# A second branch's product in seven half-size products, and gated output weights made early and kept in DRAM

## The chip, the cores and the metric

The kernel runs on one core of a Trainium2 chip. The metric is the device time of one execution in microseconds (us); a kernel's time is the median of several executions. Before the change it is 1652.44 us (three runs, 1652.39 to 1654.09).

## The reference

One layer of a two-branch backbone, with 1024 latent tokens, 256 context tokens and a model width of 1024, all in float32:

```python
pl = project(modulate(x, sh_x, sc_x), w_in)          # one wide input projection, split into 11 streams
o_gla  = bidir_gla(q, k, v, la_f, la_b, s_f, s_b)    # branch A: gated linear attention, both directions
o_diff = diff_attention(...)                         # branch B: difference of two softmaxes, 8 heads
a = merge_heads(rms_norm(o_gla) * gla_gain) * silu(gla_gate)
b = merge_heads(rms_norm(o_diff) * diff_gain * (1 - lam_init)) * silu(diff_gate)
y = sigmoid(m_gla) * (a @ w_br_gla) + sigmoid(m_diff) * (b @ w_br_diff)
x = x + g_x * (y @ w_out)
```

The change concerns `b @ w_br_diff` (the second branch's product), and `w_out` with its gate `g_x`, which the kernel multiplies into the columns of `w_out`.

## The kernel before

**Arithmetic.** A float32 product is made of three matmuls in a reduced format: each operand is split into a high part (a copy by ACT, the `ACTIVATE` rows) and a low part (a subtraction by DVE), and `mm3` adds hi·hi, hi·lo and lo·hi into one PSUM bank. A half tile of 128 x 512 outputs over the full depth of 1024 is 8 blocks of 128 by 3 matmuls, 24 in all; a full product of two 1024 x 1024 matrices is 16 half tiles, or 384 matmuls.

**Seven products.** The kernel already makes some large products from half-size blocks in seven half-size products instead of eight: both sides are cut into 2 x 2 blocks of 512, sums of blocks are formed, and seven products of these (48 matmuls each, 336 in all) are added up into the four output blocks.

**Stages.** Each stage writes what the next needs to DRAM.
- Projections (`phase_a`) fill the first half millisecond. In the paired-product stage (about 200 to 481 us; `pair_weights` and `pairs`) three groups of columns of `w_in` (`gv`, `dv`, `dg`) are made in seven products each. The token side comes from DRAM in 128 x 1280 tiles `g<-d_s`, the weights in 128 x 2 x 512 tiles `raw` and `l`; `pair_weights` forms and splits the weight sums on DVE and ACT. `direct` takes the results of one of the seven products out of PSUM.
- Gated linear attention, then the differential attention up to about 1454 us. Its scores are the `s` tiles, its transposes and value products the `b` tiles, its exponentials the `e` tiles.
- The tail, from there to the end: the second branch's product, the merge of both branches, and the output product in seven half-size products (`phase_c`).

**What sets the order.** All instruction streams are static. When the program is built, a `Driver` plays all tasks against estimated costs and writes each engine's instructions down in the order in which its model would run them, ready tasks by priority (a lower number first). All DMAs go through SP, in order; `store` queues a transfer to DRAM once its source is made. On the chip each engine follows its list and waits on semaphores. A pool tag (`raw`, `yf`, `wt`, ...) is a set of on-chip tiles; a task waits in `acq` for a free one.

**Filler.** During attention PE would wait for ACT and DVE, so `fill` lays half tiles of other products between the score and value matmuls: first gates (kind 0), then `a @ w_br_gla` (kind 1), then what it can of the second branch (kind 2). They use the PSUM banks `mb` and, from the end of the scores on, `mc`. When a half tile is done, `post` on DVE takes it out of PSUM into a tile `ft` (priority `PP`, which is -1), and only then can the bank be used again. Kind 2 is started by `first_two`, has its operand `b` split by `splits` from the tiles `wr<-d_bT`, and its results finished by `post_y`, which reads the gates and the first branch's half by `load_y`.

**Output product.** In `phase_c`, `left` makes the sums of `y` (operands `y11` to `s4`), `right` loads blocks of `w_out`, multiplies them on DVE by the gate `gb` (which made a round trip through `d_gb` in DRAM), forms their sums and splits them (`w11`, `w21`, `t2`, `t1`, `t3`, `t4`, `w22`).

In the profile L335 is a matmul, L361 a transpose on PE, L197 any operation on ACT, DVE or POOL, and L300 a DMA.

Of the kernel before, what the change touches and what calls it, by code (L numbers as in the profile page):

```python
# [20 lines left out]
P = 128  # L21
# [207 lines left out]
class Hybrid:  # L229
# [18 lines left out]
        ya=("sbC", 8), yb=("sbC", 8), yc=("sbC", 8), yf=("sbC", 16), sf=("sbC", 2), o=("sbC", 4), gbo=("sbC", 1), wr=("sbC", 8),  # L248
# [141 lines left out]
    def scratch(self):  # L390
# [13 lines left out]
        self.d_gb = d("d_gb", [P, 2, 512])  # L404
# [340 lines left out]
    def job_gate(self):  # L745
# [5 lines left out]
        for n in range(2):  # L751
# [27 lines left out]
            self.rel("p", self.pool.tensor_scalar(gb[:, n], bias, 0.5, 0.0, ALU.mult, ALU.add))  # L779
        self.store([(self.d_gb, gb)], ("gb", 1), ev=self.ev_gb)  # L780
# [139 lines left out]
    def pair_weights(self, cols, ev_load, ev_run):  # L920
# [8 lines left out]
        ev_l = {(g, n, kk): Event() for g in range(len(cols)) for n, kk, _ in LOADS}  # L929

# [12 lines left out]
        def run():  # L943
            yield ev_run
            for g in range(len(cols)):
# [31 lines left out]
                for n, o in (("t1", "w22"), ("t3", "w12"), ("t4", "w21"), ("v22", "v22")):  # L977
                    for k in range(4):
                        yield ev_l[g, o, k // 2]
                        e = yield from operand(n, k, blk(o, k))  # L980
                        if k % 2:
                            self.rel(slots[g, o, k // 2][0], e)
            d.set(self.ev_pw)

        d.spawn(load(), prio=3)
        d.spawn(run(), prio=3)
        return wp

# [146 lines left out]
    def direct(self, g, t, pm, tag):  # L1135
# [801 lines left out]
    DT = (0, 4, 1, 5, 2, 6, 3, 7)  # L1937
# [88 lines left out]
    def fill(self):  # L2026
# [4 lines left out]
               [(1, s, a["w_br_gla"][0], s * P) for s in range(8)] + \  # L2031
               [(2, s, a["w_br_diff"][0], s * P) for s in self.DT]
# [11 lines left out]
        def conv(n, raw):  # L2044
            yield self.ev_b2
            yield from self.acq("wt", 2)
            hi = self.t("wt", [P, NK, P], F32R)
# [29 lines left out]
        def half_tile(n, half, rhs):  # L2077
# [7 lines left out]
            if kind == 1:  # L2085
                yield from self.acq("ft")
                mt = self.t("ft", [P, 512])
                self.dma(mt, self.d_m[0][s][:, half * 512:(half + 1) * 512])
            elif kind == 2:
                d.spawn(self.load_y(s, half), prio=-1)  # L2090
            x = [0, None]

            def step():
# [3 lines left out]
                if k == NK - 1:  # L2097
# [40 lines left out]
        def splits():  # L2138
            r = Rhs([[[None] * 2 for _ in range(NK)] for _ in range(2)])
            r.ev = {(k, half): Event() for k in range(NK) for half in range(2)}  # L2140

            def one(k, half, x):
                yield from self.acq(f"h{half}", 2)
                hi, lo = (self.t(f"h{half}", [P, 512], F32R) for _ in range(2))
                r[0][k][half], r[1][k][half] = hi, lo
                yield d.on("ACT", x)
                self.act.activation(hi, x, AF.Copy)
                yield d.on("DVE", hi)
                e = self.dve.tensor_tensor(lo, x, hi.bitcast(F32), ALU.subtract)
                self.rel("wr", e)  # L2150
                d.set(r.ev[k, half], e)

            def run():
                yield self.ev_c2
                for half in range(2):
                    for k in range(NK):
                        yield self.ev_bT[k]
                        yield from self.acq("wr")
                        x = self.t("wr", [P, 512])
                        self.dma(x, self.d_bT[k][:, half * 512:(half + 1) * 512])  # L2160
                        d.spawn(one(k, half, x), prio=-2)
            d.spawn(run(), prio=-2)
            return r

# [6 lines left out]
        while n < len(todo):  # L2171
            kind = todo[n][0]
            one = kind == 2 or todo[n][:2] in ((1, 6), (1, 7))
            two = [n] if one else [n, n + 1]
            end = all(t[0] != kind for t in todo[n + len(two):])
            if kind == 2 and todo[n][1] == self.DT[0]:
                yield self.ev_c
                yield from self.first_two(evs[n:n + 2], (lambda m: ws[n + m]), rhs)
                n += 2
                continue  # L2180
            for half in range(2):
# [4 lines left out]
                if end:  # L2186
# [3 lines left out]
                    if half == 0 and kind == 1:  # L2190
                        nxt = splits()
            n += len(two)
            if end:
                rhs = nxt
        d.set(self.ev_fill)

    def first_two(self, evs, ws, rhs):

        d = self.d
        pms = []  # L2200
        yield self.ev_aT[7, 7, 2]
        for x in range(4):
            yield from self.acq("mc")
            pms.append(self.t("mc", [P, 512]))
        order = [(0, k, m) for m in range(2) for k in range(NK - 1)] + [(0, NK - 1, 0), (0, NK - 1, 1)]
        for half, k, m in order + [(1, k, m) for m in range(2) for k in range(NK)]:
            yield evs[m][0]
            if k == 0:
                d.spawn(self.load_y(self.DT[m], half), prio=-1)
            yield rhs.ev[k, half]  # L2210
            hi, lo = ws(m)
            e = self.mm3(pms[2 * m + half], hi[:, k], lo[:, k], rhs[0][k][half], rhs[1][k][half], k == 0, k == NK - 1)
            yield AtPE(0)
            if k == NK - 1:
                d.spawn(self.post_y("mc", self.DT[m], half, pms[2 * m + half]), d.when(pms[2 * m + half]), prio=-1)
                if half:
                    self.rel("wt", e, 2)

    def phase_b(self):
# [3 lines left out]
        self.ev_c, self.ev_c2, self.ev_s2 = Event(), Event(), Event()  # L2223
# [30 lines left out]
    def load_y(self, dt, half):  # L2254

        cs = slice(half * 512, (half + 1) * 512)
        yield self.ev_c2
        yield from self.acq("o")
        my = self.t("o", [P, 2, 512])
        self.dma(my[:, 0], self.d_m[1][dt][:, cs])  # L2260
        self.dma(my[:, 1], self.d_y[dt][:, cs])
        self.ev_my[dt, half].t_ = my
        self.d.set(self.ev_my[dt, half])

    def post_y(self, tg, dt, half, pm):

        yield self.ev_my[dt, half]
        my = self.ev_my[dt, half].t_
        yield self.d.when(my)
        e = self.dve.scalar_tensor_tensor(my[:, 0], my[:, 0], 1.0, pm, ALU.add, ALU.mult)  # L2270
        self.rel(tg, e)
        y = self.y[dt, half] = self.t("yf", [P, 512])
        e = self.dve.tensor_tensor(y, my[:, 0], my[:, 1], ALU.add)
        self.rel("o", e)
        self.d.set(self.ev_y[dt, half], e)

    def phase_c(self):
        a, d = self.a, self.d
        wo = a["w_out"][0]
        self.y = {}  # L2280
        self.ev_y = {(dt, half): Event() for dt in range(8) for half in range(2)}
        self.ev_my = {(dt, half): Event() for dt in range(8) for half in range(2)}

        def to_c():
# [9 lines left out]
            yield self.ev_gb  # L2294
            self.gb = self.t("gbo", [P, 2, 512])
            self.dma(self.gb, self.d_gb)
# [21 lines left out]
        def operand(ev, tag, src, then=()):  # L2318
# [5 lines left out]
            def run():  # L2324
# [3 lines left out]
                for f in then:  # L2328
                    f(e)
            d.spawn(run(), prio=-2)  # L2330

        def left():
# [3 lines left out]
            def take(n, tag, k, src, then=()):  # L2336
                yield from self.acq(tag, 2)
                operand(ev_l[n, k], tag, src, then)

            for k in range(4):  # L2340
                for c, n, tag in ((0, "y11", "ya"), (1, "y12", "yb")):
                    yield self.ev_y[4 * c + k, 0]
                    yield from take(n, tag, k, y(0, c, k))
                for c in range(2):
# [18 lines left out]
        def right():  # L2363

            w = {}

            def gate(n, k):
                x = w[n, k]
                self.dve.tensor_tensor(x, x, self.gb[:, int(n[2]) - 1], ALU.mult)

            def op(k, o, x, y, f):
                self.dve.tensor_tensor(w[o, k], w[x, k], w[y, k], f)

            def load(n, k, x):
                w[n, k] = x
                r, c = (int(n[1]) - 1) * 512 + k * P, (int(n[2]) - 1) * 512
                self.dma(x, wo[r:r + P, c:c + 512])

            def early():
                for k in range(4):  # L2380
                    yield self.ev_y[self.DT[k // 2], k % 2]
                    for n in ("w22", "w12"):
                        yield from self.acq("wr")
                        load(n, k, self.t("wr", [P, 512]))
                for k in range(4):
                    for n in ("w22", "w12"):
                        yield d.on("DVE", w[n, k])
                        gate(n, k)
                    op(k, "w12", "w22", "w12", sub)
                    d.set(ev_e[k])  # L2390

            ev_e = [Event() for _ in range(4)]
# [125 lines left out]
```

## Time and profile before

| | |
|---|---|
| time, median of three runs | 1652.44 us (1652.39 to 1654.09) |
| profiled execution | 1653.85 us, span 1652.1 us, mean granted TensorE clock 0.997 |
| PE busy | 1627.2 us (98%), 8389 matmuls and transposes |
| DVE, ACT, POOL busy | 1162.3 us (70%), 798.9 us (48%), 595.4 us (36%) |
| DMA | 294.44 MB, 178 GB/s over the span |

PE is TensorE's matmuls, PEld its weight loads, DVE VectorE, ACT ScalarE, POOL GpSimd, SP SyncE, which issues the DMAs. The profile is one execution; its time minus its span is what lies around the program. A row of a timeline gives start, duration, engine and operation, and in brackets the engine's idle time before it with what ended that. A row of groups gives busy time and mean duration in ns, then the idle time before. A row of windows gives busy time of each engine in a stretch of the span with the instruction count, then the granted clock, the busy share of the DMA engines, and GB/s. The chain of waits is followed back from the last instruction; its rows give start, duration and what ran.

### The profile page before, as it was taken

To read this page: it belongs to the slowest core of one execution; us is meant where nothing else is said; L and a number is where in the kernel's file an instruction comes from. 1 tells how busy PE (TensorE), PEld (TensorE's weight loads), DVE (VectorE), ACT (ScalarE), POOL (GpSimd) and SP (SyncE) were. 2 spreads that over 40 slices of the span, in tenths; PEclk is the share of its full clock that TensorE was granted. 3 is DMA by queue.
4 is the path that set the end of the run, shared out by engine and by line. 5 is a ranking of instruction groups with operands and counts; after the bars stand their busy time and mean duration, and the time that the engine had idled before them with its cause. 6 is when DMAs were issued, how large, how long until landed. Compare 5 with 4: busy or idle time off the path is not lost.

```text
span 1652.1 us, 24253 instructions
## 1 busy us (share of the span) xinstructions
PE 1627.2 (98%) x8389; PEld 1355.0 (82%) x8389; DVE 1162.3 (70%) x2019; ACT 798.9 (48%) x1640; POOL 595.4 (36%) x649
## 2 busy tenths in 40 slices
PE   8999999999999999999999999999999999999999
PEld 3788888888788888888888888888888788888887
DVE  4697853355567687687772798888888888538594
ACT  4666523343434545546442666666666656422141
POOL 1510210000146565464640455555555656600000
PEclk9999999999999999999999999999999999999999
DMA  8557857687674576546458155445356743277422
GB/s 301 180 194 260 296 212 246 235 282 272 217 227 147 176 209 183 175 148 191 116 148 232 58 130 136 118 112 135 107 139 202 225 128 97 90 233 267 154 76 77
DMA packets 248970, 294.44 MB, mean 178 GB/s; under 512 B 20712, under 2 KB 169104, under 8 KB 248848
## 3 DMA queue, kind: packets, MB, share of 16 engines
q1 hardware_dynamic: 248848, 292.90, 56.1%
q8 instruction: 66, 1.08, 0.3%
q14 instruction: 56, 0.46, 0.1%
HBM read 199.51 MB, written 93.32 MB: 177 GB/s over the span
## 4 chain that ended last, share of the span: by engine, by line
PE 88%; DVE 5%; DMA 3%; ACT 2%; issue 1%; POOL 0%; SPq 0%; DVEq 0%; ACTq 0%
PE mm L335 31%; PE mc L335 11%; PE mb L335 9%; PE s L335 8%; PE b L335 6%; PE tp L335 5%; PE b L361 4%; PE go L335 4%; PE gs L335 4%; PE gt L335 4%; DVE sm L197 2%; PE tp L361 2%; DMA raw<-in_w_in 1%; PE mz L335 1%; ACT e L197 1%
## 5 line engine op out<-in xcount | busy, mean ns | idle before, releaser
L335 PE MATMUL mm<-w,h 128*128 128x512 f32 x1260 | 318.3, 401 | 0.6 <-DVE w L197 0.4
L335 PEld LDWEIGHTS mm<-w,h 128*128 128x128 f32 x1260 | 231.8, 188 | 47.5 <-DVE w L197 1.0
L197 DVE TENSOR_REDUCE sm<-s 128x1 f32<-128x1024 f32 (+1 forms) x192 | 192.9, 1040 | 42.5 <-PE s L335 39.5
L197 ACT ACTIVATE e<-s,sm 128x1280 f32<-128x1280 f32 x128 | 170.1, 1331 | 88.4 <-DVE sm L197 68.8
L335 PE MATMUL mb<-h,wt 128*128 128x512 f32 x744 | 201.6, 406 | 0.0
L197 POOL TENSOR_SCALAR at<-ac 128x512 fp32r<-128x512 f32 x128 | 98.4, 769 | 248.1 <-ACT ac L197 225.4
L335 PE MATMUL s<-hk,aq 128*128 128x512 f32 (+1 forms) x768 | 176.1, 364 | 5.2 <-ACT e L197 4.5
L197 POOL TENSOR_TENSOR at<-ac,at 128x512 fp32r<-128x512 f32 x128 | 173.4, 1355 | 10.7
L335 PEld LDWEIGHTS mb<-h,wt 128*128 128x128 f32 x744 | 131.1, 189 | 22.5 <-ACT ft L197 0.2
L335 PE MATMUL mm<-h,w 128*128 128x512 f32 x576 | 140.1, 398 | 2.7 <-ACT p L197 0.9
L335 PEld LDWEIGHTS s<-hk,aq 128*128 128x128 f32 x768 | 121.2, 189 | 22.3 <-ACT e L197 6.0
L335 PE MATMUL mc<-h,wt 128*128 128x512 f32 x600 | 138.5, 390 | 0.0
L335 PE MATMUL b<-at,vv 128*128 128x256 f32 x960 | 132.7, 287 | 1.0 <-ACT ac L197 0.8
L335 PEld LDWEIGHTS mm<-h,w 128*128 128x128 f32 x576 | 108.2, 191 | 27.6 <-DVE w L197 1.3
L335 PEld LDWEIGHTS mc<-h,wt 128*128 128x128 f32 x600 | 111.9, 188 | 22.7
L335 PEld LDWEIGHTS b<-at,vv 128*128 128x128 f32 x960 | 121.2, 190 | 3.6 <-ACT ac L197 1.0
L197 POOL TENSOR_TENSOR sm<-sm,nhalf 128x2 f32<-128x2 f32 (+2 forms) x94 | 114.5, 1218 | 14.2 <-DVE sm L197 8.8
L197 DVE SCALAR_TENSOR_TENSOR e<-e,sm,e 128x1280 f32<-128x1280 f32 x64 | 116.8, 1824 | 1.5
L197 ACT ACTIVATE ac<-b 128x512 f32<-128x512 f32 x120 | 71.6, 598 | 82.7 <-PE b L361 82.6
L197 DVE TENSOR_TENSOR w<-raw,w 128x512 fp32r<-128x512 f32 x120 | 85.8, 737 | 30.7 <-ACT w L197 29.7
L197 ACT ACTIVATE w<-raw 128x512 fp32r<-128x512 f32 x120 | 72.3, 628 | 69.8 <-DVE raw L197 23.5
L197 POOL TENSOR_TENSOR p<-p,gdif 128x512 f32<-128x512 f32 x12 | 16.2, 1358 | 241.5 <-DVE p L197 210.4
(283 smaller groups left out, 2908.3 us busy)
## 6 DMA issues: line engine op xcount, KB each, us to landing
raw<-in_w_in SPq DMA_DIRECT2D x63, 512.0 KB, 4.5
g<-d_s SPq DMA_DIRECT2D x32, 640.0 KB, 5.5
aq<-d_qT SPq DMA_DIRECT2D x128, 128.0 KB, 3.4
d_dv<-pl SPq DMA_DIRECT2D x40, 256.0 KB, 2.2
gv<-d_v SPq DMA_DIRECT2D x40, 256.0 KB, 3.1
d_kT<-pl SPq DMA_DIRECT2D x40, 256.0 KB, 2.6
hk<-d_kT SPq DMA_DIRECT2D x32, 320.0 KB, 5.3
vv<-d_dv SPq DMA_DIRECT2D x16, 640.0 KB, 7.3
```

What stands on the lines that cost most here:

```text
L197: self.ins = f(out, *args, **kw).ins
L335: self.ins = self.nc.tensor.matmul(out, lhsT, rhs, start=start, stop=stop, skip_group_check=more).ins
L361: self.nc.tensor.transpose(out, src, self.ident[:n, :n])
```

## The change

Four things change.

1. **The second branch's product in seven.** Kind 2 leaves `fill`, and `first_two`, `splits`, `load_y` and `post_y` go. Instead `prepare` loads the blocks of `w_br_diff` (a11 to a22, rows of 2 KB) and of `b` (b11 to b22, from `d_bT`), forms eight sums for each of four blocks on DVE and splits fourteen operands for each block; `diff` runs seven products of 48 matmuls over them, taken out of PSUM by `copy` (ACT), `finish` and `rest` (DVE). The products are, in order, a11·b11, a12·b21, s2·t2, s1·t1, s3·t3, a22·t4 and s4·b22.
2. **`w_out` made early.** A new task `presums` runs in the paired-product stage, after the weight operands of the first group (two blocks), of the second (one) and of the third (one). For each block it loads four 128 x 512 pieces of `w_out`, gates them by `gb`, forms the four sums (eight DVE operations) and stores seven results to `d_pre`. In the tail `right` only loads these and splits them. `gb` stays on chip.
3. **`direct` for `dv`.** The PSUM tile is copied out by ACT first, and split from the copy.
4. **Priorities and tiles.** `post` of kind 1 goes from priority -1 to -4. `yf` has 8 tiles instead of 16, a new tag `yg` has 8, and `gbo` goes.

The core of the diff:

```diff
         ya=("sbC", 8), yb=("sbC", 8), yc=("sbC", 8),
-        yf=("sbC", 16), sf=("sbC", 2), o=("sbC", 4), gbo=("sbC", 1), wr=("sbC", 8),
+        yf=("sbC", 8), yg=("sbC", 8), sf=("sbC", 2), o=("sbC", 4), wr=("sbC", 8),
...
+    WIN = ((0, 1), (2,), (3,))
+    def presums(self, ev_win):
...
+        def out(x11, x12, x21, x22, put):
+            yield self.ev_gbt
+            for n, y in (("w11", x11), ("w21", x21), ("w22", x22), ("w12", x12)):
+                yield d.on("DVE", y)
+                dve.tensor_tensor(y, y, self.gb[:, int(n[2]) - 1], mult)
+                if n != "w12":
+                    put(n, y)
+            yield from op(x12, x22, x12, sub)
+            yield put("t3", x12, "w11")
+            yield from op(x11, x12, x11, add)
+            yield put("t2", x11, "w21")
+            yield from op(x21, x21, x11, sub)
+            yield put("t4", x21, "w22")
+            yield from op(x22, x22, x11, sub)
+            put("t1", x22)
+        for win, blocks in zip(ev_win, self.WIN):
+            yield win
+            for k in blocks:
...
+                for tag in ("l5", "x4"):
+                    yield from self.acq(tag)
+                    tiles[tag] = self.t(tag, [P, 2, 512])
...
+                for y, r, c in zip(x, (0, 0, 1, 1), (0, 1, 0, 1)):
+                    self.dma(y, src[r * 512 + k * P:r * 512 + (k + 1) * P, c * 512:(c + 1) * 512])
...
     def direct(self, g, t, pm, tag):
...
+        yield from self.acq("p")
+        x = self.t("p", [P, 512])
+        self.rel(tag, self.act.activation(x, pm, AF.Copy))
...
-        e = yield from self.split(pm, hi, lo)
-        self.rel(tag, e)
+        e = yield from self.split(x, hi, lo)
+        self.rel("p", e)
...
     def fill(self):
...
-               [(1, s, a["w_br_gla"][0], s * P) for s in range(8)] + \
-               [(2, s, a["w_br_diff"][0], s * P) for s in self.DT]
+               [(1, s, a["w_br_gla"][0], s * P) for s in range(8)]
...
-                    if kind == 2:
-                        d.spawn(self.post_y(tg, s, half, pm), e, prio=-1)
-                    else:
-                        d.spawn(post(tg, kind, s, half, pm, mt), e, prio=self.PP)
+                    d.spawn(post(tg, kind, s, half, pm, mt), e, prio=-4 if kind else self.PP)
...
+        yield self.ev_c
+        yield from self.diff()
...
+    DA = ("a11", "a12", "s2", "s1", "s3", "a22", "s4")
+    DB = ("b11", "b21", "t2", "t1", "t3", "t4", "b22")
+    ORDER = ("b11", "b12", "b22", "a12", "b21", "a21", "a22")
...
+    def prepare(self):
+        OPS = (("S1", "a21", "a21", "a22", add, ("l_a21", "l_a22"), 2), ("S2", "a11", "a21", "a11", sub, ("S1", "a11"), 2),
+               ("S4", "a12", "a12", "a11", sub, ("S2", "a12"), 4), ("S3", "a11", "a22", "a11", sub, ("S4", "s2"), 4),
+               ("T3", "b12", "b22", "b12", sub, ("l_b12", "l_b22"), 2), ("T2", "b11", "b12", "b11", add, ("T3", "b11"), 2),
+               ("T4", "b21", "b21", "b11", sub, ("T2", "b21"), 3), ("T1", "b11", "b22", "b11", sub, ("T4", "t2"), 3))
...
+    def diff(self):
...
+        todo = ((0, True, "copy", 0, 0), (1, True, "add", 0, 0), (0, False, "copy", 1, 0), (0, False, "copy", 1, 1),
+                (1, True, "keep", 1, 1), (1, False, "add", 1, 0), (0, False, "last", 0, 1))
+        for n, (b, new, what, r, c) in enumerate(todo):
+            for t in range(4):
...
+                for k in range(4):
+                    yield self.ev_d[self.DA[n], k]
+                    yield self.ev_d[self.DB[n], k]
...
+                    e = self.mm3(pm, lh[:, cs], ll[:, cs], rh, rl, k == 0 and new, k == 3, not new)
...
         def right():
+            yield self.ev_raw
+            for n in RIGHT:
                 for kk in range(2):
...
+                    self.dma(x, self.d_pre[n][:, 2 * kk:2 * kk + 2])
...
+                        operand(ev_r[n, 2 * kk + j], "h0", x[:, j])
```

The static order also shows what the diff does not. The first place is PE late in the attention, at one pair's scores (`s`), in the kernel before; `b<-ident,e` are transposes and `mb<-h,wt` filler of kind 1:

```order
L335 MATMUL s_1691_8515<-hk_8271,aq_13145 128x512 x4
L361 MATMUL b_2820_13577<-ident,e_2714_13158 128x128 x4
L335 MATMUL s_1691_8515<-hk_8271,aq_13389 128x512 x4
L361 MATMUL b_2824_13602<-ident,e_2714_13158 128x128 x4
L361 MATMUL b_2827_13611<-ident,e_2714_13158 128x128 x2
L361 MATMUL b_2830_13619<-ident,e_2735_13247 128x128 x4
L335 MATMUL mb_13635<-h_2644_12867,wt_13311 128x512
```

The same engine and place in the changed kernel, up to the middle of the stretch (the next `s`, of `aq_13488`, comes after nine more `mb` rows and four transposes):

```order
L335 MATMUL s_1704_8614<-hk_8370,aq_13244 128x512 x4
L335 MATMUL mb_13671<-h_2657_12966,wt_13410 128x512
L335 MATMUL mb_13671<-h_2658_12968,wt_13410 128x512
L335 MATMUL mb_13671<-h_2657_12966,wt_13411 128x512
L335 MATMUL mb_13671<-h_2659_12970,wt_13410 128x512
L335 MATMUL mb_13671<-h_2660_12972,wt_13410 128x512
L335 MATMUL mb_13671<-h_2659_12970,wt_13411 128x512
L361 MATMUL b_2835_13687<-ident,e_2727_13257 128x128 x4
```

Fifteen filler matmuls now stand between these two `s` groups, where none stood. The DVE rows of the same place, before; `ft<-ft,mb` is the `post` that frees the bank `mb`:

```order
L197 SCALAR_TENSOR_TENSOR e_2797_13485<-e_2803_13529,sm_13550,e_2797_13485 128x1280
L197 TENSOR_SCALAR sm_13466<-sm_13466,sm_13464 128x1
L197 TENSOR_TENSOR b1k_13534<-b_2812_13558,b1k_13534 128x256
L197 TENSOR_SCALAR sm_13562<-sm_13562,sm_13538 128x1 x2
L197 TENSOR_REDUCE sm_13574<-s_1691_8515 128x1
L197 SCALAR_TENSOR_TENSOR ft_13346<-ft_13346,mb_13345 128x512
```

And in the changed kernel:

```order
L197 SCALAR_TENSOR_TENSOR e_2794_13502<-e_2796_13511,sm_13593,e_2794_13502 128x1280
L197 SCALAR_TENSOR_TENSOR ft_13445<-ft_13445,mb_13444 128x512
L197 TENSOR_SCALAR sm_13637<-sm_12792 128x1
L197 TENSOR_SCALAR sm_13637<-sm_12882 128x1
L197 TENSOR_REDUCE sm_13564<-s_1704_8614 128x1
L197 TENSOR_TENSOR at_2821_13641<-b_2822_13642,at_2820_13640 128x2x128
```

The same `post` stands one whole pair earlier there, right behind the `e` of the pair before. The second place is SP's queue in the paired-product stage, before:

```order
L300 DMA l_458_2412<-in_w_in 128x2x512
L300 DMA g_463_2427<-d_s_245 128x1280
L300 DMA l_503_2675<-in_w_in 128x2x512
L300 DMA g_468_2454<-d_s_246 128x1280
L300 DMA raw_2458<-in_w_in 128x2x512
```

And changed:

```order
L300 DMA l_458_2417<-in_w_in 128x2x512
L300 DMA g_463_2432<-d_s_251 128x1280
L300 DMA l_464_2442<-in_w_out 128x512
L300 DMA x_465_2443<-in_w_out 128x512
L300 DMA l_464_2442<-in_w_out 128x512
L300 DMA x_465_2443<-in_w_out 128x512
L300 DMA g_470_2465<-d_s_252 128x1280
L300 DMA raw_2469<-in_w_in 128x2x512
```

Four loads of `w_out` now stand between two token-side tiles `g`, where one weight load stood; the seven stores of the block follow among the next `g` tiles, one to three at a time.

More of the change, by code (lines that the diff above doesn't have):

```diff
@@ L986, in pair_weights, with op, put @@
         d.spawn(run(), prio=3)
+        d.spawn(self.presums(ev_win), prio=3)
         return wp
+    WIN = ((0, 1), (2,), (3,))
+    def presums(self, ev_win):
+        d, dve = self.d, self.dve
+        sub, add, mult = ALU.subtract, ALU.add, ALU.mult
+        def op(o, x, y, f):
+            yield d.on("DVE", x, y)
+            return dve.tensor_tensor(o, x, y, f)
+        def out(x11, x12, x21, x22, put):
[16 more added lines that the diff above has]
+            for k in blocks:
+                src = self.a["w_out"][0]
+                tiles = {}
+                for tag in ("l5", "x4"):
+                    yield from self.acq(tag)
+                    tiles[tag] = self.t(tag, [P, 2, 512])
+                x = [tiles[tag][:, j] for tag, j in (("l5", 0), ("x4", 0), ("l5", 1), ("x4", 1))]
+                for y, r, c in zip(x, (0, 0, 1, 1), (0, 1, 0, 1)):
+                    self.dma(y, src[r * 512 + k * P:r * 512 + (k + 1) * P, c * 512:(c + 1) * 512])
+                last = []
+                def put(n, y, after=None):
+                    self.store([(self.d_pre[n][:, k], y)], ev=self.ev_pre[n, k])
+                    last.append(n)
+                    return after and self.ev_pre[after, k]
+                yield from out(*x, put)
+                for n in last:
+                    yield self.ev_pre[n, k]
+                for tag in ("l5", "x4"):
+                    self.rel(tag, d.now)
+        self.rel("gb", d.now)
+        d.set(self.ev_gb)
     def pairs(self, wp):
@@ L1934, in att_av @@
                 yield AtPE(0)
-    DT = (0, 4, 1, 5, 2, 6, 3, 7)
     PO, FI = "b1", "mb"
@@ L2136, in loads @@
             return r
[L2138 to L2163, printed above, removed]
         def pace(i):
@@ L2172, in fill @@
             kind = todo[n][0]
-            one = kind == 2 or todo[n][:2] in ((1, 6), (1, 7))
+            one = todo[n][:2] in ((1, 6), (1, 7))
             two = [n] if one else [n, n + 1]
             end = all(t[0] != kind for t in todo[n + len(two):])
[L2176 to L2180, printed above, removed]
             for half in range(2):
@@ L2316, in phase_c, with operand @@
         sub, add = ALU.subtract, ALU.add
-        def operand(ev, tag, src, then=()):
+        def operand(ev, tag, src):
             hi = self.t(tag, [P, 512], F32R)
@@ L2363, in right @@
         def right():
[L2365 to L2390, printed above, removed]
@@ L2392, in right @@
-            ev_e = [Event() for _ in range(4)]
-            d.spawn(early(), prio=3)
-            yield self.ev_loaded
-            for n in ("w11", "w21"):
-                for kk in range(2):
-                    if n == "w21" and kk:
-                        yield from self.acq("ft", 2)
-                        for k in (2, 3):
-                            load(n, k, self.t("ft", [P, 512]))
-                        continue
-                    yield from self.acq("raw")
-                    raw = self.t("raw", [P, 2, 512])
-                    for j in range(2):
-                        load(n, 2 * kk + j, raw[:, j])
@@ L2432, in phase_c, with freed @@
+        def freed(evs):
+            for ev in evs:
+                yield ev
+            self.rel("raw", d.now)
         OUT = ((0, 0), (1, 0), (1, 1), (0, 1))
```

267 lines of the change are left out of this document (185 added, 82 removed).

## The prediction

> **What bounds the kernel now.** I read the page first: engines, then the chain of waits by engine.
>
> ```profile
> PE 1627.2 (98%) x8389; PEld 1355.0 (82%) x8389; DVE 1162.3 (70%) x2019; ACT 798.9 (48%) x1640; POOL 595.4 (36%) x649
> PE 88%; DVE 5%; DMA 3%; ACT 2%; issue 1%; POOL 0%; SPq 0%; DVEq 0%; ACTq 0%
> ```
>
> PE works 98% of the span and is 88% of the chain, so time comes from taking matmuls away or from the 25 us in which PE stands still. Then the windows of the two stages that are touched, and of the busiest stretch for the DMA engines:
>
> ```profile
> 200.00:480.00 280.00, 278.43 (x1219) 228.29 (x1219) 152.65 (x223) 102.16 (x178) 23.22 (x17) 1.00 0.69 241
> 1454.00:1652.00 198.00, 194.45 (x858) 160.66 (x856) 129.30 (x196) 52.40 (x83) 0.00 (x0) 1.00 0.49 165
> 10.00:20.00 10.00, 9.15 (x21) 1.48 (x19) 2.07 (x3) 3.45 (x6) 2.26 (x6) 1.00 1.03 399
> ```
>
> In the paired-product stage PE is idle 1.6 of 280 us, in the tail only in the last 3.6 us, when the last result is written out. Both are pure PE time, at a full clock. Then the end of the chain:
>
> ```profile
> 1453.71 0.22 PE b L361 x2
> 1453.93 129.24 PE mc L335 x570
> ...
> 1637.57 10.89 PE mc L335 x48
> 1648.49 0.69 DVE wt L197
> ```
>
> After the last attention transposes (1453.71) matmuls follow each other without a gap up to 1648.5: 129.24 us for 570 is 0.2267 us each, and the 858 of the window by 0.2267 make 194.5.
>
> **The product in seven.** 384 matmuls become 336. The 48 that go are on the path, in a stretch without gaps: 48 by 0.2267 is 10.9 us. This holds for the tail as a whole, though the order also moves 21 of the matmuls behind the last transposes into the attention: 789 stand behind them, 69 fewer than the 858, and the 21 take the place of standing PE or push as much.
>
> **The stall in the attention.** The largest single wait of PE near the end of the scores is here:
>
> ```profile
> 1312.00 0.60 PE L361 MATMUL b<-ident,e 128*128 128x128 f32 x4
> 1314.49 1.73 PE L335 MATMUL s<-hk,aq 128*128 128x512 f32 x4 [1.89 <-ACT e L197]
> 1317.84 0.87 PE L361 MATMUL b<-ident,e 128*128 128x128 f32 x4 [0.34 <-ACT ac L197]
> 1318.47 0.70 PE L335 MATMUL mb<-h,wt 128*128 128x512 f32 x2
> 1299.74 1.64 PE L335 MATMUL mb<-h,wt 128*128 128x512 f32 x6
> 1306.36 2.33 DVE L197 SCALAR_TENSOR_TENSOR e<-e,sm,e 128x1280 f32<-128x1280 f32 x1
> 1309.96 1.23 DVE L197 TENSOR_REDUCE sm<-s 128x1 f32<-128x1024 f32 x1 [1.26 <-PE b L361]
> 1317.46 0.68 DVE L197 SCALAR_TENSOR_TENSOR ft<-ft,mb 128x512 f32<-128x512 f32 x1
> 1310.00:1320.00 10.00, 7.51 (x37) 5.94 (x38) 8.85 (x20) 5.97 (x16) 4.79 (x6) 0.83 0.38 119
> 1320.00:1330.00 10.00, 10.00 (x66) 8.91 (x65) 7.69 (x16) 4.91 (x13) 5.71 (x5) 1.00 0.49 142
> ```
>
> The filler in bank `mb` was finished at 1301.4 and DVE took it out only at 1317.46; for 16 us PE had no bank for filler, and at 1312.6 it ran dry for 1.89 us. In the new order this `post` stands right behind the `e` of 1306.36, so it runs at about 1308.7, in the 1.26 us for which DVE stood still, and 15 filler matmuls (3.4 us) stand between the two `s`. They cover the 1.89 us. ACT's release of the `s` bank is not made earlier by that, but it no longer matters. What would be late next is the 0.34 us at 1317.84, which I leave in.
>
> The granted clock fell with that stall: 0.83 over the 10 us, which is 1.7 us of PE time (the same `s` of four took 1.73 us there). Shorter stalls went with no drop:
>
> ```profile
> 922.73 1.19 PE L335 MATMUL s<-hk,aq 128*128 128x512 f32 x4 [1.01 <-ACT e L197]
> 916.00:926.00 10.00, 8.99 (x48) 7.32 (x47) 6.91 (x13) 6.42 (x12) 3.36 (x5) 1.00 0.07 25
> ```
>
> So I take 1.89 + 1.7 = 3.6 us for the stall gone, and bound it by 0 (it comes back elsewhere) and 4.0 (the 0.34 goes too). [...]
>
> **What the early `w_out` adds.** The paired-product stage gets 16 loads and 28 stores of 256 KB and loses the 512 KB store of `gb`: 4.2 + 7.3 - 0.5 = 11.0 MB. At the stage's share of 0.69 and the 399 GB/s of the busiest row, 280 us leave 0.31 x 280 x 399 = 34.6 MB free. DVE gets 32 instructions and is busy 152.65 of 280. On SP the four loads stand ahead of a `g` load:
>
> ```profile
> g<-d_s SPq DMA_DIRECT2D x32, 640.0 KB, 5.5
> 259.15 3.74 SPq L300 DMA_DIRECT2D g<-d_s  x2
> 265.75 2.88 PE L335 MATMUL gt<-w,g 128*128 128x512 f32 x12
> 260.00:280.00 20.00, 20.00 (x90) 16.57 (x89) 4.89 (x8) 4.14 (x7) 0.00 (x0) 1.00 0.70 249
> 280.00:300.00 20.00, 20.00 (x90) 16.54 (x89) 9.52 (x15) 5.86 (x10) 0.00 (x0) 1.00 0.75 278
> ```
>
> A `g` issued at 259.15 lands 5.5 us later, at 264.7; its first use comes about 2 us after 265.75, so about 3.1 us of cover. Four loads are 1.05 MB, 2.6 us at 399 GB/s, but one 512 KB load that stood there moves behind: 1.3 us more. That is under the cover. The seven stores (1.8 MB, 4.6 us at the same rate) are spread over five `g`. I put 0.5 us for a `g` that comes late once, with 0 below; the upper end is a rival. The copy that `direct` adds for `dv` is a few ACT operations, with ACT busy 102 of 280, and 0. DVE's other instructions in `direct` keep their number, only their source changes.
>
> [...]
>
> **Operands in the tail.** The products need more sums and splits, all on DVE and ACT. From the order DVE has 239 instructions behind the last transposes, against 196 in the window. Their step:
>
> ```profile
> 1583.38 1.89 DVE L197 TENSOR_TENSOR h<-raw,h 128x512 fp32r<-128x512 f32 x3
> wr<-d_bT SPq DMA_DIRECT2D x16, 256.0 KB, 5.7
> 1454.00:1520.00 66.00, 66.00 (x293) 54.62 (x291) 38.30 (x55) 19.33 (x28) 0.00 (x0) 1.00 0.84 280
> 1580.00:1600.00 20.00, 20.00 (x89) 16.55 (x89) 19.90 (x34) 9.64 (x17) 0.00 (x0) 1.00 0.12 45
> ```
>
> Three take 1.89 us, with starts 0.6 apart: 239 by 0.6 is 143 us of the 179 (789 by 0.2267) that PE needs. DVE was full for 20 us at 1580 and PE missed nothing, so a full DVE alone costs nothing; late operands do. Two places are narrow. (a) The third product of the branch, s2·t2, starts 48 us behind the last transposes. Its operands wait for 31 transfers of 256 KB, 8.1 MB, 29 us at the 280 GB/s of that window, then 5.7 for the last to land and nine DVE steps of 0.6: 40 us, 8 us of slack. (b) The third product of the output, where from the last tile of the second sum on DVE has 31 instructions, 18.6 us, with about 1.8 us of waits for ACT, in 21.8 us of PE: 1.4 us of slack. I put 0.7 us there, half of what a late operand by 1.4 us would cost; below is 0. The `w_out` gates and sums, once 32 instructions of DVE in the tail, are gone from it and counted in the 239. The loads of `right` become 14 of 512 KB in place of 16 of 256 KB, in a stretch with a DMA share of 0.12 (1580 to 1600), and cost 0.
>
> **Sum.** -10.9 - 3.6 + 0.5 + 0.7 = -13.3 us. The profiled execution took 1653.85 us (span 1652.1), 1.4 above the median of 1652.44, and none of the terms lies in that difference; against the profiled one it gives 1640.5, and against the median **1639.1 us**, 0.8% faster. A measurement of this kernel can tell about 0.2%, 3.3 us.
>
> **The rivals.**
> - *The stall comes back.* Filler moved ahead is filler missing later: the same wait for ACT `e` could appear two pairs on. For it: PE's filler is used up sooner, and 21 matmuls are drawn from behind the attention. Against: the new order has those 21 to draw from. 1639.1 + 3.6 = 1642.7.
> [...]
> - *Late operands in the tail.* PE waits about 2 us at one to three product starts, each with a dip like that of 1314.49 (3.6 us together). For it: place (b), and DVE at 80% of the tail. Against: 8 us at place (a). 1638.4 plus 3.6 to 10.8: 1642 to 1649.
> - *The paired-product stage becomes bound by DMA*, the one that ends slower. If the 2.9 MB of each block's loads and stores come in a lump ahead of a `g`, that is 7.2 us at 399 GB/s, less 3.1 of cover, and 1.7 for a dip: 5.8 us for each of four blocks, 23 us, 1638.6 + 23.2 = 1662. It ends slower than before from 17.1 us exposed on. For it: `g` tiles arrive 5.5 us after issue, not far ahead of use. Against: 0.31 of the DMA engines' time is free, and the stores are spread.
>
> That the change doesn't do what it says speaks only in the first: the number of matmuls is fixed by the static program.
>
> **How the numbers follow.** The forecast 0.52, with its own range 1636.8 (both costs 0, the 0.34 gone, the median's spread) to 1641.5; the clock 0.08; the stall back 0.15; late operands 0.14, of which 0.02 within 0.2% of before; DMA 0.11, of which 0.03 within and 0.08 slower. Faster: 0.52 + 0.08 + 0.15 + 0.12 = 0.87; same 0.05; slower 0.08. The range goes from 1636.8 to 1648.5 and takes in all but the DMA case and the edge of the late operands.
>
> **What would show it.** In the profile after: 8341 PE instructions, of them 789 behind the last transposes at the same 0.2267 us; no wait of 1.89 us and a clock of 1.00 where 0.83 was; the pairs' stage with a DMA share near 0.8 and PE still idle under 3 us; the last transposes at about 1453.9 - 3.6 + 4.8 (the 21 moved ahead) + 0.5 = 1455.6. Waits of PE on DVE splits behind 1455, or on `g<-d_s` between 240 and 480, would show the forecast wrong and say which rival it is.

## The result, and the profile after

The changed kernel takes 1638.79 us (median of six runs, 1637.48 to 1641.75) against 1653.48 (six runs, 1652.39 to 1654.09): 14.7 us less, a ratio of 0.9915 with a 95% interval of 0.9902 to 0.9928. The forecast was 1639.1, or 13.3 us less than the 1652.44 that three runs had given for the kernel before.

The page of the changed kernel, engines and the chain by engine:

```profile
span 1637.5 us, 24388 instructions
PE 1610.8 (98%) x8341; PEld 1342.3 (82%) x8341; DVE 1204.6 (74%) x2095; ACT 819.1 (50%) x1689; POOL 596.2 (36%) x649
PE 88%; DVE 5%; DMA 2%; ACT 2%; issue 2%; POOL 1%; SPq 0%; ACTq 0%; DVEq 0%
```

PE has 48 instructions fewer, 8341 for 8389; it is still 98% busy and 88% of the chain. The windows of the paired-product stage and of the tail, and the chain of the tail:

```profile
200.00:480.00 280.00, 276.37 (x1211) 226.76 (x1210) 170.31 (x253) 103.98 (x180) 23.43 (x16) 1.00 0.78 277
1454.00:1637.00 183.00, 179.51 (x792) 148.05 (x790) 149.44 (x240) 70.12 (x127) 0.00 (x0) 1.00 0.55 191
...
1454.12 0.22 PE b L361 x2
1454.34 37.44 PE mc L335 x165
...
1578.82 2.05 PE mc L335 x9
1580.88 0.68 DVE yc L197
1581.55 0.04 issue
1581.60 19.56 PE mc L335 x85
...
1622.91 10.89 PE mc L335 x48
1633.83 0.69 DVE wt L197
```

The tail is one row of matmuls again, broken once: at 1581.60 PE came 0.28 us late for a DVE split (`yc`), at the third product of the output, place (b) of the forecast. In the paired-product stage PE is idle 3.6 us where it was 1.6. The waits behind that, and the place of the old stall, in PE's timeline and the windows:

```profile
450.80 3.69 PE L335 MATMUL tp<-w,g 128*128 128x512 f32 x15 [2.25 <-DMA g<-d_s]
1311.22 0.74 PE L335 MATMUL s<-hk,aq 128*128 128x256 f32 x4 [0.54 <-ACT e L197]
1312.95 1.55 PE L335 MATMUL mb<-h,wt 128*128 128x512 f32 x6
1317.31 1.08 PE L335 MATMUL s<-hk,aq 128*128 128x512 f32 x4
1420.62 0.98 PE L335 MATMUL mb<-h,wt 128*128 128x512 f32 x3 [1.23 <-DVE ft L197]
1310.00:1320.00 10.00, 9.46 (x53) 7.75 (x52) 8.02 (x18) 6.95 (x16) 5.49 (x6) 1.00 0.50 144
440.00:445.00 5.00, 5.00 (x24) 4.14 (x23) 1.55 (x3) 1.71 (x3) 0.00 (x0) 1.00 1.05 381
445.00:450.00 5.00, 3.54 (x16) 2.61 (x14) 3.78 (x6) 2.46 (x5) 0.00 (x0) 1.00 1.06 391
```

The kernel before in the last of these windows:

```profile
445.00:450.00 5.00, 5.00 (x24) 4.10 (x23) 1.20 (x2) 3.55 (x6) 0.00 (x0) 1.00 1.03 388
```

The stall of 1.89 us is gone, filler (`mb`) stands in it, and the granted clock is 1.00 there. Two waits are new: 2.25 us for a token-side tile `g` at 450, with the DMA engines full at 381 to 391 GB/s for 10 us, and 1.23 us for `ft`. The engines were full there before the change too (388 GB/s), but no tile was late.

The two profiled spans differ by 14.6 us, like the medians. But the profile of before has a slow clock early on that the profile of after has not (last section), so stage times are compared below between runs that had no such dip.

### The profile page after: what moved, and what is told of

Read it like the earlier page. It is cut to its first block, busy times and chain, and to the rows that moved or that the text cites. A ratio compares the mean times of both kernels' runs of the same rounds, so it can differ in the third digit from the quotient of the medians.

```text
span 1637.5 us, 24388 instructions
## 1 busy us (share of the span) xinstructions
PE 1610.8 (98%) x8341; PEld 1342.3 (82%) x8341; DVE 1204.6 (74%) x2095; ACT 819.1 (50%) x1689; POOL 596.2 (36%) x649
## 4 chain that ended last, share of the span: by engine, by line
PE 88%; DVE 5%; DMA 2%; ACT 2%; issue 2%; POOL 1%; SPq 0%; ACTq 0%; DVEq 0%
PE mm L335 30%; PE mb L335 9%; PE mc L335 9%; PE s L335 8%; PE b L335 7%; PE tp L335 5%; PE b L361 4%; PE go L335 4%; PE gt L335 4%; PE gs L335 3%; PE mz L335 2%; DVE sm L197 2%; PE tp L361 2%; ACT e L197 1%; DMA g<-d_s 1%
## 5 line engine op out<-in xcount | busy, mean ns | idle before, releaser
L335 PE MATMUL mb<-h,wt 128*128 128x512 f32 x816 | 220.9, 405 | 1.2 <-DVE ft L197 1.2
L335 PEld LDWEIGHTS mb<-h,wt 128*128 128x128 f32 x816 | 144.0, 189 | 26.2 <-DVE ft L197 1.5
L197 ACT ACTIVATE p<-mm 128x512 f32<-128x512 f32 (+1 forms) x107 | 61.6, 584 | 78.8 <-PE mm L335 65.4
L361 PE MATMUL b<-ident,e 128*128 128x128 f32 x604 | 93.7, 272 | 0.0
```

The lines of the kernel that those rows point to most:

```text
L197: self.ins = f(out, *args, **kw).ins
L335: self.ins = self.nc.tensor.matmul(out, lhsT, rhs, start=start, stop=stop, skip_group_check=more).ins
L361: self.nc.tensor.transpose(out, src, self.ident[:n, :n])
```

## The experiments

Each was timed in five rounds beside the kernel before on its own chip. Differences are to the kernel before there (1653.4, 1653.38 and 1653.24 in the three groups) unless another is named.

**1. The place of `post` alone**, in the kernel before:

```diff
-                        d.spawn(post(tg, kind, s, half, pm, mt), e, prio=self.PP)
+                        d.spawn(post(tg, kind, s, half, pm, mt), e, prio=-4 if kind else self.PP)
```

> The kernel before with one edit of the change: post of kind 1 at priority -4. Its matmul count is that of before; in its static order 21 filler matmuls move ahead of the last transposes, as in the changed kernel. Theory A (the forecast's: the late post of the bank mb makes the stall at 1314, and the clock's dip belongs to that stall): the whole attention gain of the two traces, 5.3 us (1.89 + 0.34 of waits, 1.7 of clock, the rest small waits), so 1648.2 against 1653.5. Theory B (the clock's dips are drawn run by run, not tied to this stall): waits alone, 3 to 3.6 us in the median, 1650.2, and the runs still differ by 1 to 2 us with their mean granted clock. Theory C (the post's place is not what removed the stall): 0.

Measured: 1648.5 us, -4.9, ratio 0.9972 (0.996 to 0.9983). One number gives a third of the gain. In its profile the stall is gone and the 1.25 us wait for `ft` is there as in the changed kernel. The interval, 2.8 to 6.6 us, takes in theory A's 5.3 as well as the 3 to 3.6 of B, so the size alone does not choose; the next two runs speak against A's reason, the clock.

**2. The same line put back in the changed kernel:**

```diff
-                    d.spawn(post(tg, kind, s, half, pm, mt), e, prio=-4 if kind else self.PP)
+                    d.spawn(post(tg, kind, s, half, pm, mt), e, prio=self.PP)
```

> The changed kernel with post of kind 1 back at priority -1. The same 21 matmuls go back behind the last transposes. Theory A: the stall of about 1.9 us at the same pair of scores returns with a clock below 1.00 in its window, +5.3 us, 1644.1. Theory B: the stall returns, the clock's dip only in some runs, +3 to +3.6, 1642.2. Theory C: no change.

Measured: 1660.86 us, 22 above the changed kernel and slower than before (ratio 1.0045, 1.0033 to 1.0058). No theory had that. Its PE and DVE timelines:

```profile
1314.08 1.19 PE L335 MATMUL s<-hk,aq 128*128 128x512 f32 x4 [1.54 <-ACT e L197]
1516.24 5.37 PE L335 MATMUL mc<-h,wt 128*128 128x512 f32 x12 [15.67 <-DVE ft L197]
...
1501.42 2.49 DVE L197 TENSOR_TENSOR wr<-yc,wr 128x512 f32<-128x512 f32 x4
1509.85 2.48 DVE L197 TENSOR_TENSOR raw<-yb,raw 128x512 f32<-128x512 f32 x4
1515.51 0.68 DVE L197 SCALAR_TENSOR_TENSOR ft<-ft,mc 128x512 f32<-128x512 f32 x1
1510.00:1520.00 10.00, 3.76 (x9) 2.99 (x10) 6.72 (x11) 1.26 (x2) 0.00 (x0) 0.50 0.39 131
```

The old stall returned, 1.54 us, as expected. But PE also stood still for 15.67 us at 1500, for one `ft` at 1515.51: DVE was busy throughout, above all with the sums and splits of the new product (`wr`, `raw` and others), whose priorities of -3 to -2.4 are better than -1, so that they were written down ahead of it. PE needs the bank that this `ft` empties. The 0.50 of the granted clock behind it adds to the price. So the new product needs the new priority; without it the change as a whole loses.

**3. The early `w_out` alone**, in the kernel before: `presums`, the `right` that reads `d_pre`, and the new `direct`; the second branch keeps 384 matmuls.

> The kernel before with the early w_out alone (presums, gb kept on chip, right loading from d_pre, the new direct); the second branch's product stays at 384 matmuls and PE's order is row for row that of before. Theory D1 (the traces: one token-side tile comes 2.25 us late at the fourth block, nothing else): +2.5 us, 1656.0, with a PE wait on DMA g<-d_s near 450. Theory D2 (the forecast's term): +0.5, 1654.0, the wait of 2.25 us being a chance of the profiled run. Theory D3 (the forecast's DMA rival): +17 or more. That DVE is relieved in the tail is worth 0 in all three, since PE has no gap there in the kernel before.

Measured: 1654.62 us (eleven runs), +1.2, ratio 1.0008 (1.0 to 1.0017), between D1 and D2. Its PE timeline:

```profile
450.60 3.68 PE L335 MATMUL tp<-w,g 128*128 128x512 f32 x15 [1.81 <-DMA g<-d_s]
1311.20 0.74 PE L335 MATMUL s<-hk,aq 128*128 128x256 f32 x4 [0.54 <-ACT e L197]
1315.08 1.19 PE L335 MATMUL s<-hk,aq 128*128 128x512 f32 x4 [1.55 <-ACT e L197]
1353.88 2.40 PE L335 MATMUL b<-at,vv 128*128 128x256 f32 x18 [0.77 <-ACT ac L197]
```

The late `g` is there again, 1.81 us: no chance of one run, but a cost of the early `w_out`. Experiment 1's profile passes the `s` of 1311.20 at 1308.91, after as many matmuls, so by these two profiles the early part costs 2.3 us, inside the interval of the medians (0 to 2.8).

**4, 5. The fourth block of `w_out` later, and sooner.** In the changed kernel a block does not wait for all the operands of its group: the fourth starts after the second of four `t4` operands, the others after the second `t3`. Later: started after the last weight operand of the third group. Sooner: in the second group, behind the third block.

```diff
-                        if (n, k) == (("t3", 1), ("t3", 1), ("t4", 1))[g]:
+                        if (n, k) == (("t3", 1), ("t3", 1), ("v22", 3))[g]:
```

```diff
-    WIN = ((0, 1), (2,), (3,))
+    WIN = ((0, 1), (2, 3), ())
```

> The changed kernel with the fourth block of w_out started after the last weight operand of the third group instead of after t4, so three of its loads and all its stores stand behind the last token-side tiles of that product. Theory D1: the wait for g<-d_s of 2.25 us at 450 goes, 1636.5 against 1638.8. Rival: the DMA engines are full there anyway (388 GB/s at 445 to 450 in the kernel before too) and a wait of over 1 us stays, 1638; or the later stores hold up the loads of the next stage, a new wait between 470 and 500, 1639 or more.

> The changed kernel with the fourth block of w_out made right after the third, in the second group of weights, where its loads stand among stores of d_dv and not ahead of a token-side tile. PE's order is row for row that of the changed kernel. If the wait of 2.25 us for g<-d_s at 450 is the fourth block's traffic and its place has room, it goes: 1636.5 against 1638.8. If the DMA engines have no room between 360 and 400 either, a wait for g<-d_s or for weights of 1 to 3 us comes there: 1638.8 to 1641.

Measured: 1643.1 and 1644.17 us, 4 to 5 slower than the changed kernel. Their PE waits, of the later one first:

```profile
449.36 3.65 PE L335 MATMUL tp<-w,g 128*128 128x512 f32 x15 [0.71 <-DMA g<-d_s]
482.49 15.30 PE L335 MATMUL mm<-w,h 128*128 128x512 f32 x66 [1.68 <-DVE p L197]
645.25 0.73 PE L335 MATMUL mm<-w,h 128*128 128x512 f32 x2 [1.44 <-DVE w L197]
653.05 1.44 PE L335 MATMUL mm<-w,h 128*128 128x512 f32 x5 [1.37 <-DVE w L197]
```

```profile
434.45 4.50 PE L335 MATMUL mm<-w,g 128*128 128x512 f32 x9 [5.83 <-ACT w L197]
432.32 0.69 DVE L197 TENSOR_TENSOR raw<-x,raw 128x512 f32<-128x512 f32 x1 [4.55 <-DMA raw<-in_w_in]
426.57 1.05 SPq L300 DMA_DIRECT2D raw<-in_w_in  x1
```

The late tile shrank to 0.71 in the one and went in the other. In its place came waits of 1.4 to 1.7 us further on, and one of 5.83 us for weights whose load was issued at 426.57 and kept DVE waiting for 4.55. The first halves of both expectations fail. The rivals hold in kind; the second came out larger than its rival had it (1 to 3 us, up to 1641).

**6. A product twice.** The first of the seven products runs twice, the second pass starting the sums anew; its operands come free after the second pass:

```diff
-                for k in range(4):
+                for i, k in enumerate((0, 1, 2, 3) * (2 if n == 0 else 1)):
...
-                    if t == 3:
+                    if t == 3 and (n or i > 3):
```

> The changed kernel with the first of the seven products of the second branch run twice into the same banks (the second pass starts the sum anew): 48 matmuls more, no other work. Theory T1 (a matmul in this stretch costs its 0.2267 us, since nothing stands): +10.9, 1649.7. Theory T2 (operands of the second and third product are about as late as PE is early, so that part of the 48 matmuls' time is bought back elsewhere): under +9.

Measured: 1650.18 us (eleven runs), 11.4 above the changed kernel: T1. From the first matmul behind the last transposes to the end its profile takes 1647.4 - 1453.45 = 193.9 us, the changed kernel's 183.4: 10.5 more. A matmul in the tail costs its step; of the 10.9 us only about the 0.28 of the wait for `yc` comes back, which this profile does not have.

**7. The loads of `w_out` twice**, the same data:

```diff
                     self.dma(y, src[r * 512 + k * P:r * 512 + (k + 1) * P, c * 512:(c + 1) * 512])
+                    self.dma(y, src[r * 512 + k * P:r * 512 + (k + 1) * P, c * 512:(c + 1) * 512])
```

> The changed kernel with each of the 16 early loads of w_out issued twice (4.2 MB more; the same data). Theory D1 (the DMA engines are full around the late tile, 381 to 391 GB/s): each block's four extra loads are 1.05 MB, 2.7 us; the wait at 450 grows from 2.25 to about 5 and one or two of the other three blocks show a late tile: +3 to +8, 1642 to 1647. Theory D4 (the tile was late through its place in SP's queue or by chance, not through the bytes): within 1 us of 1638.8.

Measured: 1661.96 us, 23 above the changed kernel and slower than before (ratio 1.0049, 1.0037 to 1.0062). PE's timeline and one window:

```profile
267.82 0.94 PE L335 MATMUL gt<-w,g 128*128 128x512 f32 x3 [1.33 <-DMA g<-d_s]
272.44 1.62 PE L335 MATMUL gt<-w,g 128*128 128x512 f32 x3 [3.68 <-DMA g<-d_s]
374.43 6.42 PE L335 MATMUL tp<-w,g 128*128 128x512 f32 x15 [3.86 <-DMA g<-d_s]
471.03 5.94 PE L335 MATMUL tp<-w,g 128*128 128x512 f32 x15 [7.08 <-DMA g<-d_s]
360.00:380.00 20.00, 16.14 (x60) 12.72 (x59) 7.94 (x12) 5.41 (x9) 0.00 (x0) 0.84 0.97 357
```

Waits of 16 us for `g`, in all three groups of weights, and clock dips with them (0.84 here, 0.83 at 260 to 280 and at 460 to 480): late tiles as D1 had them, well over its size. But the edit does more than add bytes. Its second copy writes the same tile as the first, and SP, which issues in order, waits for the first to land. SP's waits between 200 and 480 us (total, number, longest), and the chain ahead of the wait of 7.08:

```profile
SPq L300 <- DMA l<-in_w_out: 11.1, 8, 4.3
SPq L300 <- DMA x<-in_w_out: 5.9, 8, 3.0
...
458.88 4.05 DMA x<-in_w_out
463.85 7.04 DMA g<-d_s
```

SP stood 17.0 us in all for these copies, and at the fourth block one of them is itself on the chain. Ahead of the waits of 3.68 and 3.86 the `g` tiles took 9.92 and 9.38 us from issue to landing, against a median of 5.5 in the kernel before, so there the transfers were slow. That late `g` tiles can lose all that the change gained is shown; how much of the 23 us is bytes, and how much the standing queue that D4 names, is not.

**8. The old `direct`** in the changed kernel: `dv` split straight from PSUM.

```diff
-        yield from self.acq("p")
-        x = self.t("p", [P, 512])
-        self.rel(tag, self.act.activation(x, pm, AF.Copy))
         yield from self.acq("pl", 2)
...
-        e = yield from self.split(x, hi, lo)
-        self.rel("p", e)
+        e = yield from self.split(pm, hi, lo)
+        self.rel(tag, e)
```

> The changed kernel with direct for dv as before (split from PSUM, no copy by ACT). PE's order is unchanged. Every theory has 0 here; a bank of that product freed about 0.6 us later could cost up to 0.6 a tile where PE waits for it, which no wait of the kernel before shows: 1638.8 to 1639.4.

Measured: 1647.05 us, 8.3 above the changed kernel. All theories fail. ACT's and PE's timelines and PE's windows:

```profile
405.02 0.60 ACT L197 ACTIVATE pl<-mm 128x512 fp32r<-128x512 f32 x1 [2.68 <-DMA d_dv<-pl]
405.04 4.61 PE L335 MATMUL mm<-w,h 128*128 128x512 f32 x12 [3.62 <-DVE pl L197]
400.00:420.00 20.00, 16.38 (x66) 13.09 (x65) 9.65 (x15) 5.64 (x10) 1.30 (x1) 0.91 0.66 244
440.00:460.00 20.00, 17.81 (x73) 14.28 (x72) 12.21 (x21) 10.09 (x19) 0.00 (x0) 0.93 0.99 349
```

The split needs a free pair of `pl` tiles, and these come free only when the stores `d_dv<-pl` have gone out. ACT waits 2.68 us for one, the PSUM bank stays full, and PE waits 3.62 us for the bank. The copy to `p` cuts that tie. The kernel before splits from PSUM too, and ACT has no such wait there; the DMA engines carry 300 and 238 GB/s at 395 to 400 and 400 to 405 in it, 396 and 367 here. So the traffic of `w_out` is the likely reason why the store is late; no run separates it from the new order of SP's queue. Two clock dips (0.91 and 0.93 of 20 us, 1.8 and 1.4 us) are part of the 8.3; the second follows a late `g` of 2.19 us, which the changed kernel has as well.

**9 to 11. The changed kernel again, and the fourth block a little sooner** within its group, after `t3` and after `t1`:

```diff
-                        if (n, k) == (("t3", 1), ("t3", 1), ("t4", 1))[g]:
+                        if (n, k) == (("t3", 1), ("t3", 1), ("t3", 1))[g]:
```

> The changed kernel unaltered, on the chip of the next two, so that they can be compared with it: 1638.8, 14.6 below before.

> The changed kernel with the fourth block of w_out started after the third group's t3 operand, four weight operands sooner; its four loads then stand together ahead of one token-side tile and the first stores one tile earlier. PE's order is unchanged. If the late tile at 450 comes from this block's bytes falling between 440 and 450, where the DMA engines were full before the change too, moving part of them toward 435 to 440 (share 0.6 to 0.8) shortens the wait of 2.25 us by 1 us or more: 1636.5 to 1637.8. If the bytes only push another transfer late (as in the two runs that moved the block further), it stays or grows: 1639 to 1644.

> The same with the start after the third group's t1 operand, the earliest place tried: all four loads stand ahead of a load of the group's own weights. If room in the DMA engines decides: no late tile at 450, 1636.5. If the weights it passes come late: a PE wait for ACT or DVE on w near 430 to 445 of several us, 1641 to 1645.

Measured: 1639.73 (ratio 0.992, 0.9908 to 0.9933), 1639.62 and 1640.84 us. The result repeats; the shifts bring nothing that the spread lets one see. Neither reason of experiment 11 holds: the late tile stays, and PE's waits for weights from 420 to 450 come to 0.9 us. The late tile is in all three:

```profile
449.60 5.13 PE L335 MATMUL tp<-w,g 128*128 128x512 f32 x15 [2.39 <-DMA g<-d_s]
```

```profile
451.41 3.69 PE L335 MATMUL tp<-w,g 128*128 128x512 f32 x15 [2.13 <-DMA g<-d_s]
450.00:455.00 5.00, 3.59 (x16) 2.98 (x17) 2.40 (x4) 0.63 (x1) 0.29 (x1) 1.00 1.05 404
```

```profile
451.55 5.28 PE L335 MATMUL tp<-w,g 128*128 128x512 f32 x15 [2.49 <-DMA g<-d_s]
```

In the second the DMA engines stay full to 455, at 404 GB/s. No version beat the changed kernel. Why the fourth block's move does not free the tile stays open.

## Why the prediction was right

Experiment 1 gives -4.9 and experiment 3 +1.2; the whole is -14.6 against 1653.4, so -10.9 is left for the product in seven, which is the term of the forecast. That is a remainder of three medians, each uncertain by 1.4 to 2.2 us, and experiment 2 shows that the parts are not independent. The profiles say the same more closely: from the first matmul behind the last transposes to the end experiment 1 takes 1646.0 - 1451.76 = 194.2 us and the changed kernel 1637.5 - 1454.09 = 183.4, 10.8 less.

- **The product in seven, -10.9:** right, and shown by the 10.8 of the profiles and by experiment 6 (+11.4 for 48 matmuls, 10.5 by its profile).
- **The stall, -3.6:** right in mechanism, -4.9 measured, but the working was off. The clock term of 1.7 us need not come with the stall: experiments 2 and 3 have it, 1.54 and 1.55 us long, and the window around it at a clock of 1.00. Nor was it 1.7 in the kernel before: from the `s` of 1310.26 to the first matmul behind the last transposes its profile takes 143.43 us, and experiment 3, with the same matmuls there, 142.48; 0.95 us is all that the dip and the longer stall cost. What the working missed is what 21 more filler matmuls do. From the `s` of 1311 to the first matmul behind the last transposes experiment 3 takes 142.48 us, the changed kernel 142.87 with 21 more matmuls, 4.76 us of work for 0.39. That gains 4.4 us without any clock term. PE's idle time there falls from 3.84 to 1.47 us, for the stall and smaller waits are filled (0.37, 0.50 and 0.77 in experiment 3); the other 2 us are gained in stretches that the profile counts as busy, and it does not show how. The forecast had those 21 down as neutral.
- **The early `w_out`, +0.5:** mis-sized, +1.2 by the median and 2.3 by the profiles. The cover was worked out at one tile, at 259, and that tile came in time. The late one was at the fourth block, at 450, where the DMA engines were already full before the change (a share of 1.03 at 445 to 450). The stage's mean share of 0.69 hid that.
- **`direct`, 0:** the sum was right and the reading wrong. The copy is no small extra; without it the early `w_out` costs 8.3 us more (experiment 8).
- **The priority** was costed in the attention only. In the tail it keeps `ft` ahead of the new sums, worth 15.67 us of PE time and a clock dip there (0.50 over 10 us, experiment 2).
- **The tail, +0.7:** about right in place and size; one wait at place (b), of 0.28 us in this profile and 0.61 in that of experiment 9, and none at (a).
- **The rivals.** The stall did not come back, though a wait of 1.23 us for `ft` did. The slower rival, late `g` tiles in a stage bound by DMA, was the real danger. One of its waits came, 2.25 us at 450, which is a sign that the prediction had named against itself; so is PE's idle time of 3.6 us in that stage, which was to stay under 3. In experiment 7 such waits came in all three groups, though in part through SP's queue. The clock's dip, which has 0.08 among the chances, did not stay when the stall went: 1.00 where 0.83 was. How long PE must stand for it no run shows: stalls of 1.54 and 1.55 us in experiments 2 and 3 left the clock at 1.00, and in experiment 9 a wait of 2.39 us was followed by 0.73 from 450 to 455.

The narrow miss of 0.3 us is in good part luck. The forecast change was -13.3 and the measured one -14.7, a miss of 1.4; but the forecast started from the median of three runs, 1652.44, and six runs put the kernel before at 1653.48, which hides 1.0 of it. The terms were off both ways: 1.3 us too little gain for the stall, 0.7 too little cost for the stage, 0.4 too much cost for the tail, 1.0 in all, and the rest is within the spread.

## What to carry to other kernels

When PE is full, count matmuls by their step in the stage itself; that term was the surest here (10.9 us forecast, 10.8 by the profiles). Look for the cover of extra DMA traffic at the fullest few microseconds, not in the stage's mean (here a share of 1.03 against 0.69), and at everything that waits for the queue: the loads behind, the tiles that stores set free, and the PSUM banks that wait for these tiles. And when a new task goes onto a shared in-order engine, check which old instruction it now stands ahead of: here two small edits beside the main one, a priority and a copy, held off losses of 22 and 8 us. When a test run adds traffic, check that it does not also make the queue wait, as SP's did for 17.0 us in experiment 7.

## What the runs showed of the hardware

The granted clock falls in some runs and not in others, behind nearly the same gap. The windows of 45 to 55 us, before and after, lie in the projections, ahead of both stages that the change alters:

```profile
45.00:50.00 5.00, 3.48 (x26) 3.02 (x25) 3.74 (x8) 5.00 (x10) 2.86 (x6) 0.86 0.74 216
50.00:55.00 5.00, 4.43 (x12) 3.18 (x11) 5.00 (x7) 1.44 (x3) 2.72 (x3) 0.50 0.83 219
```

```profile
45.00:50.00 5.00, 3.48 (x26) 2.34 (x25) 3.74 (x9) 5.00 (x10) 2.59 (x6) 1.00 0.84 248
50.00:55.00 5.00, 3.95 (x17) 3.00 (x17) 5.00 (x7) 1.67 (x3) 2.99 (x3) 1.00 0.95 248
```

PE was busy 3.48 us of the first 5 in both, and only the kernel before was then held to 0.50. In the changed kernel the wait at 450 ended in 3.69 us for 15 matmuls in the one profile (after 2.25 us) and in 5.13 in the other (after 2.39), 1.4 us more. Over the changed kernel's first six runs the mean granted clock goes from 1.000 to 0.997 and the time from 1637.48 to 1641.75 us. Over all the profiles with the early `w_out` but that of experiment 7, the 15 matmuls behind waits for this tile of 0.71, 1.68, 1.81, 1.99, 2.13 and 2.25 us took 3.65 to 3.69 us, those behind 2.19, 2.39 and 2.49 us took 5.25, 5.13 and 5.28 (the clock was 0.73 and 0.75 over 5 us for the last two, 0.93 over 20 us for the first). So a gap of some 2 us cost its length and, in some profiles, 1.4 to 1.6 us more; the longer ones more often, but 2.19 and 2.25 stand the wrong way round. What decides it is left open.
